# The last sort stage in two halves: the second half of the edges is finished between the one-hots of the first

## The chip, the cores and the metric

The kernel runs on one core of a Trainium2 chip. Its time is the device time of one execution in microseconds (us), as the median of several runs; a profile of one execution is read beside it. The engines are PE (matrix products), DVE (vector), ACT (activations, copies out of PSUM), POOL (here mostly issuing DMAs) and SP (issuing DMAs).

## What is computed

A graph layer without its nonlinearity: 4096 nodes of 256 features and 262,144 edges.

```python
self_out = nodes @ w_self
msg = nodes[edges_src] @ w_msg
agg = zeros(N, D); np.add.at(agg, edges_dst, msg)
return self_out + agg
```

As `nodes[src] @ w_msg` is row `src` of `Y = nodes @ w_msg`, the work is `A @ Y + nodes @ w_self`, where `A[dst, src]` counts the edges from `src` to `dst`. The kernel builds the counts `A` in tiles and multiplies them.

## The kernel before

**Load and key (L155 to L182).** The edges come in as 128 rows of 2048. DVE makes one f32 key of each edge: its destination segment (11 of them, 374 nodes each), its source block (32 blocks of 128 nodes), the destination in the segment and the source in the block. A pair of segment and block is called a run; there are 352.

**First sort (`SORT_A`, `_Sort.run`, tiles XA).** A network of compare-exchange passes along the rows. One pass is a `min` and a `max` on DVE (`_Sort.mm`, L634). Between groups of passes PE rotates columns across partitions (L777), and ACT copies the result back (L781). The last rotation of the list is applied by the transposes that follow.

**Last sort stage (`SORT_S`, tiles XS, L823 to L847).** PE transposes 28 blocks of 128 x 128, and ACT copies them to XS (L834), so that partition q holds columns 16q to 16q+15 of the sorted order, 2048 elements, with a halo of 768 of its neighbours' elements on either side. 16 passes then run along the partition, each narrower than the last, with no exchange between partitions. `_tail_plan` works out the ranges, and `waves` starts the first two passes on the part that has already come. Ahead of these passes PE and ACT are given the projection `Y` (L230), which runs beside them.

**Bases and places (L257 to L306).** For each of the 2048 columns of 128 sorted edges DVE finds the smallest key (`k16`, `gi`), and subtracts this base from the column's keys (`rel`). PE transposes `rel` (L280), and ACT turns it into 16-bit `vals`, one column of 128 edges per free index (L283). DVE works out from `gi` in which PSUM bank and at which offset each column's counts go (`poff`); 10 small steps. An ACT pass sums whatever falls outside the width W (L304).

**Main loop (L464 to L512).** It goes over the 2048 columns, and the order of the instructions on every engine is the order of the Python text (`manual_schedule`). For each block of columns (8, 8, 16, 32, 32, 32, then 64 each) DVE writes two one-hot tiles, `e_oh` (source in block, 128 wide) and `d_oh` (destination, W = 112 wide), with three buffers each (L333 to L352): one subtraction (L344) and then one comparison for every 16 values of the width (L349). For each column PE multiplies the two and adds the product at a run-time offset in a ring of six PSUM banks:

```python
count_mm(
    ring[:, bass.ds(off, W)], e[:, ci // 2, :, ci % 2], d[:, ci // 2, :, ci % 2], False
)
```

The keys are near enough to sorted that run r falls between two straight lines in the column number: `CLEAR` says at which column its bank is cleared (L384, it waits for the copy out of run r-6), and `EVAC` at which column ACT copies it to SBUF (L393). 46 columns later three products with `Y` add it to `out_ps` (L438 to L442). Where a count falls over the end of its segment, POOL adds the overhang to the next run by an accumulating DMA (`merge`, L411). After 32 runs a segment of the output is complete; ACT copies it to one of two `o_sb` buffers, and SP stores it in pieces, each of which waits for a later run's copy (L507).

**Check (L515 to L541).** The bases are written to DRAM and read back shifted by one (`kd`, `kn`, on SP), and DVE sees whether any column lies outside what the ring can hold. If one does, a general path is taken (`_any_edges`); on the data of this case it is not. These steps stand behind the manual order; they are placed where the scheduler puts them: in the program before, SP issues both DMAs ahead of all stores, and DVE runs the steps (L523 to L531) between the first blocks of one-hots.

Of the kernel before, what the change touches and what calls it, by code (L numbers as in the profile page):

```python
# [9 lines left out]
P = 128  # L10
# [12 lines left out]
W = 112  # L23
GAP = W - 8
NB = 32
JB = 16
NSEG = 11
# [36 lines left out]
    ('q', 2, [64, 91, 42, 124, 107, 2, 87, 24, 28, 87, 6, 7, 86, 49, 10, 1]),  # L64
# [12 lines left out]
def kernel(  # L77
# [17 lines left out]
    G16 = NCOL // P  # L95

# [14 lines left out]
    nc.gpsimd.iota(col_i[:], pattern=[[1, G16]], base=0, channel_multiplier=G16)  # L111
# [12 lines left out]
    TOT = NCOL + 2 * halo  # L124
# [22 lines left out]
    muladd(lom_c[:], lo_c[:], 683, 0)  # L147
    tss(out=lom_c[:], in_=lom_c[:], scalar=12, op=ALU.logical_shift_right)
    muladd(lom_c[:], lom_c[:], RING, -OFF)
    muladd(hi_c[:], hi_c[:], 1, -OFF)  # L150
# [90 lines left out]
    sort = _Sort(nc, tc, psum_sort, XA, XS, id2, zw)  # L241
    own = sort.run(plan, halo, project)

    def col16(name, dt):
# [9 lines left out]
    junk = meta.tile([P, NCOL], BF16, name="junk")  # L254
    bcol = meta.tile([P, 2], FP32, name="bcol")

    other = XS[0] if own is XS[1] else XS[1]  # L257
    own = own[:, halo:halo + NCOL]
    rel = other[:, 0:NCOL]
    assert SORT_S[-1] == (8, 1)  # L260
    low8 = own.rearrange("p (c i t b) -> p c i t b", i=8, t=2, b=8)
    sort.note(
        nc.vector.tensor_reduce(out=k16[:], in_=low8[:, :, :, 1, :], axis=AX.XY, op=ALU.min), NCOL // 2
    )
    sort.note(
        nc.vector.tensor_reduce(out=kmin[:], in_=low8[:, :, 0, 0, :], axis=AX.X, op=ALU.min), NCOL // 16
    )
    sort.note(tt(out=k16[:], in0=k16[:], in1=kmin[:], op=ALU.min), G16)
    sort.note(tss(out=gi[:], in_=k16[:], scalar=7, op=ALU.arith_shift_right), G16)
    sort.warm(len(sort.log), 2.4, 9)  # L270
    for t in range(G16 // 4):
        tp = psum_sort.tile([P, 512], FP32, name="tp_sw", tag="tp", bufs=4)
        s4 = slice(4 * t * P, 4 * (t + 1) * P)
        stt(
            out=_view3(rel[:, s4], P), in0=_view3(own[:, s4], P), scalar=1.0 / P,
            in1=gi[:, 4 * t:4 * t + 4].unsqueeze(2).to_broadcast([P, 4, P]),
            op0=ALU.mult, op1=ALU.subtract,
        )
        for k in range(4 * t, 4 * t + 4):
            nc.tensor.transpose(  # L280
                tp[:, (k % 4) * P:(k % 4 + 1) * P], rel[:, k * P:(k + 1) * P], ident[:]
            )
        nc.scalar.activation(  # L283
            out=vals[:].rearrange("p (q k) -> p q k", k=G16)[:, :, 4 * t:4 * t + 4],
            in_=tp[:].rearrange("p (k q) -> p q k", k=4),
            func=ACTF.Relu, scale=-float(P), bias=top[:],
        )
    muladd(rho[:], gi[:], 1.0 / SW, 0.5 / SW - 0.5)
    stt(out=dl[:], in0=rho[:], scalar=float(-SW), in1=gi[:], op0=ALU.mult, op1=ALU.add)
    tt(out=rhoc[:], in0=rho[:], in1=lo_c[:], op=ALU.max)  # L290
    tt(out=rhoc[:], in0=rhoc[:], in1=hi_c[:], op=ALU.min)
    tt(out=sl[:], in0=rhoc[:], in1=lom_c[:], op=ALU.subtract)
    nc.vector.tensor_scalar(
        out=wr[:], in0=sl[:], scalar1=float(RING), scalar2=float(-RING * BW),
        op0=ALU.is_ge, op1=ALU.mult,
    )
    stt(out=wr[:], in0=sl[:], scalar=float(BW), in1=wr[:], op0=ALU.mult, op1=ALU.add)
    tt(out=poff[:], in0=wr[:], in1=dl[:], op=ALU.add)
    nc.vector.tensor_scalar(
        out=poff[:], in0=poff[:], scalar1=2, scalar2=PSUM0,  # L300
        op0=ALU.logical_shift_left, op1=ALU.bitwise_or,
    )
    sort.keep_warm(10)
    nc.scalar.activation(  # L304
        out=junk[:], in_=vals[:], func=ACTF.Relu, scale=-1.0, bias=limit[:], accum_out=bcol[:, 1:2],
    )  # L306
# [16 lines left out]
    split_at = {0: 64, 64: 512, 512: 1280, 1280: NCOL}  # L323
# [4 lines left out]
    def onehots(c, n):  # L328
        res = []
        if c in split_at:  # L330
            split_vals(c, split_at[c])
        for nm, val, wid, row in (("e", slo_b, P, jrow), ("d", rel_b, W, drow)):
            o = ohp.tile([P, 32, wid, 2], BF16, name=nm + "_oh", tag=nm, bufs=3)  # L333
            v = val[:, c:c + n].rearrange("p (g i) -> p g i", i=2).unsqueeze(2)
            if n < 32:
                shp = [P, n // 2, wid, 2]
                tt(
                    out=o[:, 0:n // 2], in0=v.to_broadcast(shp),
                    in1=row[:].unsqueeze(1).to_broadcast(shp), op=ALU.is_equal,
                )  # L340
            else:
                u = ohp.tile([P, 32, JB, 2], I16, name=nm + "_off", tag="off", bufs=2)
                shp = [P, n // 2, JB, 2]
                tt(  # L344
                    out=u[:, 0:n // 2], in0=v.to_broadcast(shp),
                    in1=row[:, 0:JB, :].unsqueeze(1).to_broadcast(shp), op=ALU.subtract,
                )
                for j in range(0, wid, JB):
                    tss(  # L349
                        out=o[:, 0:n // 2, j:j + JB, :], in_=u[:, 0:n // 2], scalar=float(-j),  # L350
                        op=ALU.is_equal,
                    )  # L352
            res.append(o)
        return res
# [28 lines left out]

    def clear(r):  # L384
        b = (r % RING) * BW
        after = [evac_of[r - RING]] if r >= RING else []
        zone = bass.AP(
            tensor=ring.tensor, offset=ring[:, b:b + 1].offset,
            ap=[list(ring[:].ap[0]), [SW + W - GAP, 2], [1, GAP]],
        )  # L390
        count_mm(zone, zer[:, 0, :], zer[:, 1:3, 0:GAP], True, after)

    def evac(r):  # L393
        at = ats[r % NAT]
        b = (r % RING) * BW
        ins = nc.scalar.copy(out=at[:, 0:SW + W], in_=ring[:, b:b + SW + W]).ins  # L396
        tc.declare_no_dep(
            ins, group="count", keep=[last_mm[0]], reason="disjoint banks by static schedule"
        )
        tc.add_manual_dep(ins, last_mm[0].name, DEP, reason="run complete")  # L400
        tc.add_to_no_dep_group("evac", ins)
        evac_of[r] = ins
        at_of[r] = at
# [60 lines left out]
    if True:  # L464
# [3 lines left out]
        nev = 0  # L468
        starts = {}
# [4 lines left out]
        for c in range(NCOL):  # L474
            if c in starts:
                c0 = c
                e, d = onehots(c, starts[c])
            ci = c - c0
            while ncl < NRUN and clear_at(ncl) <= c:
                clear(ncl)  # L480
                ncl += 1
            if c % 8 == 0:
                regs = [nc.tensor.alloc_register(f"po{c}_{i}") for i in range(8)]
                nc.tensor.load(regs, poff[c // G16:c // G16 + 1, c % G16:c % G16 + 8])
# [33 lines left out]
    bsum = meta.tile([1, 2], FP32, name="bsum")  # L518
    btot = meta.tile([1, 1], FP32, name="btot")
    flag = meta.tile([1, 1], I32, name="flag")  # L520
    nc.sync.dma_start(kd[0, 0:NCOL].rearrange("(p g) -> p g", g=G16), k16[:])
    nc.sync.dma_start(kn[:], kd[0, 1:NCOL + 1].rearrange("(p g) -> p g", g=G16))
# [9 lines left out]
    nc.tensor.matmul(out=ring[0:1, 0:2], lhsT=onesc[:], rhs=bcol[:], start=True, stop=True)  # L532
    nc.vector.tensor_copy(out=bsum[:], in_=ring[0:1, 0:2])  # L533
    tt(out=btot[:], in0=bsum[:, 1:2], in1=bsum[:, 0:1], op=ALU.add)
    nc.vector.tensor_single_scalar(out=flag[:], in_=btot[:], scalar=0.0, op=ALU.is_gt)
    ohp.release()
    psum2.release()
# [62 lines left out]
def _tail_plan(passes):  # L600

    a, e = 0, 2048
# [10 lines left out]
    halo = -(-max(-a, e - 2048) // 128) * 128  # L613
# [8 lines left out]
class _Sort:  # L622
    def __init__(self, nc, tc, psum, XA, XS, id2, zw):
        self.nc, self.tc, self.psum = nc, tc, psum
        self.XA, self.XS, self.id2, self.zw = XA, XS, id2, zw
        self.log = []
        self.turn = 0

# [3 lines left out]
    def mm(self, out, in0, in1, op):  # L632
        self.note(
            self.nc.vector.tensor_tensor(out=out, in0=in0, in1=in1, op=op),  # L634
            out.ap[1][1] * out.ap[2][1],
        )
# [149 lines left out]
    def run(self, plan, halo, project):  # L786
# [36 lines left out]
        u, v = self.XS  # L823
        nk = (2048 + 2 * halo) // P
        for t in range(0, nk, 4):
            w = min(4, nk - t)
            tp = self.psum.tile([P, 512], FP32, name="tp_sw", tag="tp", bufs=4)
            for k in range(t, t + w):
                c = k - halo // P
                nc.tensor.transpose(  # L830
                    tp[:, (k - t) * P:(k - t + 1) * P],
                    x[:, FP + c:FP + c + 16 * (P - 1) + 1:16], self.turned(last[c // 2 % 8]),
                )
            nc.scalar.copy(out=u[:, t * P:(t + w) * P], in_=tp[:, 0:w * P])  # L834
        project()
        waves = []
        for end in (1024, 2048):
# [7 lines left out]
        return self.passes(  # L845
            u, v, [q[0:2] for q in plan], halo, [q[2:4] for q in plan], waves
        )[0]  # L847
# [30 lines left out]
```

## Time and profile before

| what | number |
|---|---|
| median of 5 runs | 484.07 us (483.16 to 486.45) |
| profiled execution | 487.51 us, of which the span of the profile is 485.7 |
| mean granted PE clock | 0.943 |
| first sort, DVE XA group (142 instructions) | 97.1 us busy |
| last sort stage, DVE XS group (40 instructions) | 131.7 to 178.3 us |
| first one-hot on DVE | 184.6 us |
| one-hot products on PE (2048) | 186.6 to 474.8 us |

In a group of the page, the columns are line, engine, operation, output and input with partitions x elements, count; then busy us and mean ns of one; then the idle time of the engine just before and what ended most of it. In a table of windows, each engine has its busy us and count, and behind them stand the granted PE clock (1.00 is full), the share of the DMA engines and GB/s. In a list of waits: who waited for whom, us in total, times, longest. In a timeline: start, length, engine, line, operation, count.

### The profile page before, as it was taken

The page shows a single profiled execution, that of the slowest core. Times are in us where ns is not written, and L with a number is a line of the kernel's source. Part 1 is how long each engine was busy: PE and PEld are TensorE (multiplying, and loading weights), DVE is VectorE, ACT ScalarE, POOL GpSimd, SP SyncE. Part 2 cuts the span into 40 slices and gives each one's busy share as a digit, 9 for nine tenths or more (in the row PEclk, how much of TensorE's full clock was granted, in tenths as well). Part 3 has the DMA queues.
Part 4 walks back from the last instruction along what each step waited for, and adds up shares of the span by engine and source line. Part 5 has one row for each costly group of instructions (what it writes and reads, how often), then busy time and mean ns, then how long its engine had stood idle before and what let it go on. Part 6 is the DMA issues. An engine that isn't in the chain of part 4 may idle for free.

```text
span 485.7 us, 10912 instructions
## 1 busy us (share of the span) xinstructions
PE 373.9 (77%) x4086; PEld 305.7 (63%) x4095; DVE 402.2 (83%) x834; ACT 239.2 (49%) x454; POOL 195.6 (40%) x190
## 2 busy tenths in 40 slices
PE   0009746989870039989999999989999999989994
PEld 0004231655440015779888989879898899988893
DVE  6999999899899999999988768787988688986400
ACT  3100010322271005567676767667676677767772
POOL 4200000000000000566766577666667675766760
PEclk9999786999996559999999999999999999999998
DMA  8894111111000000334544444453545454545351
GB/s 323 117 168 119 27 24 27 26 25 27 11 0 0 0 1 2 26 27 38 52 40 51 42 49 44 46 50 40 53 42 55 39 55 39 56 38 54 37 58 43
DMA packets 66016, 23.90 MB, mean 49 GB/s; under 512 B 51882, under 2 KB 64682, under 8 KB 65962
## 3 DMA queue, kind: packets, MB, share of 16 engines
q0 software_dynamic: 43872, 10.57, 26.4%
q1 hardware_dynamic: 21260, 10.42, 8.1%
q10 hardware_dynamic: 830, 2.20, 1.2%
q8 instruction: 33, 0.54, 0.5%
q14 instruction: 21, 0.17, 0.1%
HBM read 8.92 MB, written 6.30 MB: 31 GB/s over the span
## 4 chain that ended last, share of the span: by engine, by line
PE 48%; DVE 29%; issue 7%; POOL 6%; DMA 6%; ACT 2%; SPq 0%; POOLq 0%; DVEq 0%; ACTq 0%
PE ring L372 20%; PE out_ps L439 18%; DVE XA L634 14%; DVE XS L634 10%; POOL atr L416 6%; PE warm L671 6%; DMA atr<-atr 4%; PE tp_sw L777 2%; DMA d<-in_edges_dst_dram 2%; PE out_ps L434 1%; PE out_ps L428 1%; DVE e_oh L349 1%; DVE d_oh L349 1%; ACT atr L396 1%; ACT XA L781 1%
## 5 line engine op out<-in xcount | busy, mean ns | idle before, releaser
L416 POOL DMA_DIRECT2D atr<-atr x163 | 186.9, 1269 | 267.7 <-ACT atr L396 264.6
L396 ACT CAST atr<-ring 128x486 bf16<-128x486 f32 x352 | 192.9, 567 | 89.7 <-PE ring L372 68.7
L372 PE MATMUL ring<-d_oh,e_oh 128*128 128x112 bf16 x2048 | 193.2, 213 | 8.7 <-issue 4.6
L439 PE MATMUL out_ps<-Y,atr 128*128 128x256 bf16 x1056 | 170.0, 272 | 4.6 <-DMA atr<-atr 4.2
L372 PEld LDWEIGHTS <-e_oh 128*128 128x128 bf16 x2048 | 162.0, 97 | 15.6 <-issue 6.4
L349 DVE TENSOR_SCALAR e_oh<-e_off 128x1024 bf16<-128x1024 int16 (+1 forms) x264 | 98.7, 444 | 39.0 <-PE ring L372 38.1
L671 PE MATMUL warm<-zw 128*128 128x512 bf16 x169 | 56.7, 432 | 86.5 <-DVE XA L634 50.9
L634 DVE TENSOR_TENSOR XA<-XA 128x510 f32<-128x510 f32 (+35 forms) x142 | 97.1, 732 | 6.2 <-ACT XA L781 4.5
L439 PEld LDWEIGHTS <-atr 128*128 128x128 bf16 x1056 | 89.3, 97 | 13.4 <-DMA atr<-atr 5.5
L671 PEld LDWEIGHTS <-zw 128*128 128x128 bf16 x176 | 17.8, 104 | 121.5 <-issue 59.4
L372 PE MATMUL ring<-zer 128*128 128x208 bf16 x352 | 88.3, 251 | 0.1
L349 DVE TENSOR_SCALAR d_oh<-d_off 128x1024 bf16<-128x1024 int16 (+1 forms) x231 | 87.1, 446 | 1.1
L781 ACT COPY XA<-tp_sw 128x512 f32<-128x512 f32 x24 | 14.2, 592 | 93.3 <-PE tp_sw L777 92.6
L634 DVE TENSOR_TENSOR XS<-XS 128x512 f32<-128x512 f32 (+17 forms) x40 | 46.0, 1196 | 2.6 <-ACT XS L834 2.0
L372 PEld LDWEIGHTS <-zer 128*128 128x128 bf16 x352 | 34.0, 97 | 3.6 <-ACT atr L396 1.5
L777 PEld LDWEIGHTS tp_sw<-XA,id 128*128 128x128 f32 x192 | 22.5, 190 | 3.3 <-ACT XA L781 1.7
L777 PE MATMUL tp_sw<-XA,id 128*128 128x128 f32 x192 | 23.4, 276 | 1.2 <-DVE XA L634 1.2
L344 DVE TENSOR_TENSOR e_off<-slo_b,jrow 128x1024 int16<-128x1024 int16 (+1 forms) x33 | 21.5, 653 | 0.0
L344 DVE TENSOR_TENSOR d_off<-rel_b,drow 128x1024 int16<-128x1024 int16 (+1 forms) x33 | 21.5, 652 | 0.0
L533 DVE COPY bsum<-ring 1x2 f32<-1x2 f32 x1 | 0.1, 148 | 24.1 <-PE ring L532 24.1
L283 ACT ACTIVATE vals<-tp_sw,top 128x512 int16<-128x512 f32 x4 | 2.4, 688 | 34.5 <-PE tp_sw L280 34.5
L434 PE MATMUL out_ps<-Y,atr 128*128 128x256 bf16 x65 | 17.6, 271 | 0.0
(95 smaller groups left out, 141.7 us busy)
## 6 DMA issues: line engine op xcount, KB each, us to landing
atr<-atr POOLq DMA_DIRECT2D x123, 56.0 KB, 2.8
out_dram<-o_sb SPq DMA_DIRECT2D x110, 32.0 KB, 1.5
nodes_bf<-in_nodes_dram POOLq DMA_DIRECT2D x1, 2048.0 KB, 16.3
nodes_bf_dram<-nodes_bf SPq DMA_DIRECT2D x1, 2048.0 KB, 8.7
atr<-atr POOLq DMA_DIRECT2D x40, 28.0 KB, 2.8
s<-in_edges_src_dram ACTq DMA_DIRECT2D x2, 512.0 KB, 8.8
d<-in_edges_dst_dram SPq DMA_DIRECT2D x2, 512.0 KB, 6.2
XT<-nodes_bf_dram SPq DMA_TRANSPOSE x64, 2.4
```

Of the source, the lines that this page charges most:

```text
L344: tt(out=u[:, 0:n // 2], in0=v.to_broadcast(shp), in1=row[:, 0:JB, :].unsqueeze(1).to_broadcast(shp), op=ALU.subtract,)
L349: tss(out=o[:, 0:n // 2, j:j + JB, :], in_=u[:, 0:n // 2], scalar=float(-j), op=ALU.is_equal,)
L372: mm = nc.tensor.matmul(out=ap, lhsT=lhsT, rhs=rhs, start=start, stop=True, skip_group_check=True,).ins
L396: ins = nc.scalar.copy(out=at[:, 0:SW + W], in_=ring[:, b:b + SW + W]).ins
L416: nc.gpsimd.dma_start(out=atr[:, b:b + n, 0:W], in_=atr[:, a:a + n, SW:SW + W], accum_op=ALU.add)
L428: nc.tensor.matmul(out=out_ps[0:m, t, :], lhsT=XT[:, k, c0:c0 + m], rhs=wcat[:, k, :], start=(k == 0 and t % 2 == 0), stop=False, skip_gro ...
L434: nc.tensor.matmul(out=out_ps[:, 0, :], lhsT=spill[:, SW:SW + P], rhs=Y[:, b, :], start=False, stop=False, skip_group_check=True,)
L439: nc.tensor.matmul(out=out_ps[:, t, :], lhsT=at[:, t * P:(t + 1) * P], rhs=Y[:, b, :], start=False, stop=(b == NB - 1), skip_group_check=True,
L634: self.nc.vector.tensor_tensor(out=out, in0=in0, in1=in1, op=op),
L671: self.nc.tensor.matmul(out=w[:], lhsT=self.zw[:, 0:P], rhs=self.zw[:], start=True, stop=True).ins
L777: self.nc.tensor.matmul(out=tp[:, g * P:(g + 1) * P], lhsT=self.turned(rots[8 * h + 4 * t + g]), rhs=sel(x)[:, 4 * t + g], start=True, sto ...
L781: self.nc.scalar.copy(out=sel(y)[:, 4 * t:4 * t + 4], in_=tp[:].rearrange("p (g i b) -> p g i b", g=4, b=bb),)
```

## The change

The last sort stage is done in two halves of 1024 columns. Each half is transposed to its own pair of tiles with its own halos of 768 (20 blocks each: XS, and the new XL), so that partition q holds columns 8q to 8q+7 of the half. The passes of the first half stay where they were. Those of the second are kept as a list of 32 instructions, which are issued four at a time after the one-hots of each block from column 256 on. After the one-hots of block 768 the second half's bases and subtractions follow; its transposes go to one bank of the ring, which is lent out between runs 147 and 148, in the middle of the columns 857 and 872; the later runs all move on by one bank (`bank`, `bank_free`). The second half's places are worked out ahead of block 960, and its values are split at column 1024.

```diff
-W = 112
+W = 110
+HALF = 1024
+SHIFT = 148
+LATE_FROM = 256
+LATE_STEP = 4
+LATE_SUB = 768
+LATE_TURN = 872
+LATE_USE = 960
...
-    ('q', 2, [64, 91, 42, 124, 107, 2, 87, 24, 28, 87, 6, 7, 86, 49, 10, 1]),
+    ('q', 2, [103, 74, 61, 94] * 4),
...
-    TOT = NCOL + 2 * halo
+    TOT = HALF + 2 * halo
+    latep = tc.alloc_tile_pool(name="latep", bufs=1)
+    XL = [latep.tile([P, TOT], FP32, name=f"XL{i}") for i in range(2)]
...
+            if self.h == 0:
+                stt(
+                    out=sl[:, c], in0=rhoc[:, c], scalar=float(SHIFT - OFF), in1=sl[:, c],
+                    op0=ALU.is_ge, op1=ALU.add,
+                )
...
-    split_at = {0: 64, 64: 512, 512: 1280, 1280: NCOL}
+    split_at = {0: 64, 64: 512, 512: HALF, HALF: HALF + 256, HALF + 256: NCOL}
...
+    def bank(r):
+        return (r + (r >= SHIFT)) % RING * BW
+
+    def bank_free(slot):
+        old = slot - RING
+        if old == SHIFT:
+            return [late_read[-1]]
+        return [evac_of[old - (old > SHIFT)]] if old >= 0 else []
...
+    def turn_late(t):
+        b = bank(SHIFT - 1) // BW
+        b = (b + 1) % RING * BW
+        mms, act = late.turn(t, ring[:, b:b + BW])
+        for m in mms:
+            after = bank_free(SHIFT) if t == 0 else [late_read[-1]]
...
     def clear(r):
-        b = (r % RING) * BW
-        after = [evac_of[r - RING]] if r >= RING else []
+        b = bank(r)
+        after = bank_free(r + (r >= SHIFT))
...
+                if c == LATE_USE:
+                    late.places()
                 e, d = onehots(c, starts[c])
+                if c >= LATE_FROM:
+                    for _ in range(LATE_STEP):
+                        if rest:
+                            rest.pop(0)()
+                if c == LATE_SUB:
+                    assert not rest
+                    late.bases()
+                    for t in range(2):
+                        late.subtract(t)
+            if c == LATE_TURN:
+                turn_late(1)
+                late.total()
             ci = c - c0
             while ncl < NRUN and clear_at(ncl) <= c:
+                if ncl == SHIFT:
+                    turn_late(0)
                 clear(ncl)
...
-    nc.sync.dma_start(kd[0, 0:NCOL].rearrange("(p g) -> p g", g=G16), k16[:])
-    nc.sync.dma_start(kn[:], kd[0, 1:NCOL + 1].rearrange("(p g) -> p g", g=G16))
+    for h in range(2):
+        nc.sync.dma_start(
+            kd[0, h * HALF:(h + 1) * HALF].rearrange("(p g) -> p g", g=G8), k16[:, h * G8:(h + 1) * G8]
+        )
+    for h in range(2):
+        nc.sync.dma_start(
+            kn[:, h * G8:(h + 1) * G8],
+            kd[0, h * HALF + 1:(h + 1) * HALF + 1].rearrange("(p g) -> p g", g=G8),
+        )
...
+        own = self.passes(*self.XS[0], ps, halo, spans, waves)[0]
+        self.defer = []
+        self.passes(*self.XS[1], ps, halo, spans, [])
+        late, self.defer = self.defer, None
```

`late.turn(t, tp)` transposes four blocks of 128 x 128 f32 on PE into `tp` and lets ACT write `vals` from it, `late.bases` is the two reductions and two small steps of L262 to L269, `late.subtract(t)` is one instruction of L274, `late.places` the small steps of L288 to L302, and `late.total` the sum of L304 over one half. In the built program the second half's check steps (`gn` and `v`) stand on DVE within block 832, the others within the places at block 960; on SP, the first half's `kd` stands ahead of all stores, and the second half's `kd` and both `kn` after the third store of the third segment.

## The prediction

> **What bounds the kernel now.** I read the page first.
>
> ```profile
> PE 373.9 (77%) x4086; PEld 305.7 (63%) x4095; DVE 402.2 (83%) x834; ACT 239.2 (49%) x454; POOL 195.6 (40%) x190
> ...
> PE 48%; DVE 29%; issue 7%; POOL 6%; DMA 6%; ACT 2%; SPq 0%; POOLq 0%; DVEq 0%; ACTq 0%
> ...
> L349 DVE TENSOR_SCALAR e_oh<-e_off 128x1024 bf16<-128x1024 int16 (+1 forms) x264 | 98.7, 444 | 39.0 <-PE ring L372 38.1
> ...
> L634 DVE TENSOR_TENSOR XS<-XS 128x512 f32<-128x512 f32 (+17 forms) x40 | 46.0, 1196 | 2.6 <-ACT XS L834 2.0
> ```
>
> DVE is busiest, yet PE holds the chain. Two stages with different limits explain it. The table by windows:
>
> ```profile
> 150.00:160.00 10.00, 0.00 (x0) 0.00 (x0) 9.90 (x8) 0.00 (x0) 0.00 (x0) 0.52 0.00 0
> 160.00:170.00 10.00, 0.00 (x0) 0.00 (x0) 9.86 (x9) 0.00 (x0) 0.00 (x0) 0.50 0.00 0
> ...
> 220.00:260.00 40.00, 38.69 (x514) 35.88 (x511) 37.63 (x97) 28.92 (x54) 26.61 (x24) 1.00 0.45 44
> 260.00:300.00 40.00, 38.12 (x504) 34.92 (x503) 30.52 (x76) 27.59 (x52) 27.22 (x24) 1.00 0.48 48
> ```
>
> From 131.7 to 178.3 us the last sort stage runs on DVE with nothing beside it: every microsecond removed there is one of the span. From 186.6 to 474.8 PE is nearly full, and DVE is idle a quarter of the time only from about 260 us; before, it is full. The waits say the same: DVE waits for PE to free one-hot buffers, PE hardly waits for DVE.
>
> ```profile
> DVE e_oh L349 <- PE ring L372: 38.1, 23, 3.5
> ...
> PE ring L372 <- DVE d_oh L349: 2.8, 2, 2.0
> ```
>
> The sum hangs on how far DVE is ahead when the late sort begins. From the DVE timeline:
>
> ```profile
> 178.22 1.21 DVE L263 TENSOR_REDUCE k<-XS 128x16 int32<-128x1024 f32 x1
> ...
> 180.08 2.50 DVE L274 SCALAR_TENSOR_TENSOR XS<-XS,gi 128x512 f32<-128x512 f32 x4
> ...
> 189.35 0.17 DVE L523 TENSOR_SCALAR gn<-kn 128x16 int32<-128x16 int32 x1
> ...
> 216.77 0.68 DVE L344 TENSOR_TENSOR e_off<-slo_b,jrow 128x1024 int16<-128x1024 int16 x1
> ...
> 224.11 0.68 DVE L344 TENSOR_TENSOR e_off<-slo_b,jrow 128x1024 int16<-128x1024 int16 x1
> ```
>
> The line at 216.77 opens the one-hots of block 256 (columns 256 to 319); they end at 224.18. Counting the 2048 one-hot products on PE, column 256 starts at 227.32: a lead of 3.1 us. The leads at blocks 320, 384, 448, 512 and 832 are 4.6, 6.8, 9.7, 10.2 and 11.4 us. So the idle 38 us belong to a DVE that already has its three buffers full, which is later than where the late sort is put.
>
> **Ahead of the first one-hot.** The pass pairs fit n/0.96 ns plus 0.131 us (n = 1040: 1.160 and 1.269 us from start to start). Every one of the 16 passes loses 1024 elements (3584 to 2560 columns with halos) and the instructions stay 40: 16,384 x 1.0417 ns = 17.07 us. The reductions halve: 0.53 + 0.07. Two of four subtractions go: 1.25; the address steps stay ten on DVE (the added bank-shift step replaces one check that ran there), and two ACT turnings still end before them. Sum 18.9 us, all on the path. The 12 more transposes and 3 more ACT copies come ahead of the projection, which ended at 147.2; with 10 x 0.5 us of ACT instead of 7 it ends near 149, under a sort that now ends at 161. If that cover were gone they would cost 1.5 us.
>
> The first blocks are bound by DVE (leads 0.05 us at columns 64 and 128). Five small check steps (the line at 189.35 and four like it) leave this stretch: 0.8 us. d one-hots of 110 save 0.2. Block 256's one-hots therefore end at 224.18 - 19.9 = 204.3.
>
> **The late sort.** 23,408 elements x 1.0417 ns + 32 x 0.131 = 28.6 us, in eight portions of four instructions after the one-hots of blocks 256 to 704: 5.3, 4.7, 3.8, 3.4, 3.2, 3.0, 2.8, 2.7. A one-hot block takes DVE 6.96 us (mean distance of five starts from 202.89 to 237.69), 6.93 at the new width; PE takes 8.2 to 9.9. So DVE gains some 2 us a block on PE and the portions take more. The lead of 3.1 us is gone at block 320 (3.1 + 8.2 - 12.2 = -0.9). From there to block 832 DVE sets the time, with PE idle by about 0.9, 3.0, 2.3, 2.6, 1.7, 1.5, 1.2, 1.2 us a block.
>
> After block 768 come the late reductions and subtractions, 2.5 us, and then a new wait. gn (after block 832's e_off) needs kn, which needs kd's second half: in the trace kn's last packet landed 2.7 us after k was done; one more issue ahead of it (0.33) makes 3.1, of which 2.1 pass in DVE work. I take 1.0 us; bounds 0 and 2.5, if busy DMA doubles the landings. Behind it on DVE stand the one-hots of block 832, for which PE waits. On SP, the second kd and both kn stand ahead of nine stores of the third segment: these are held until k is done, some 120 columns, then go in a burst; their buffer is not needed before column 989, so 0, or up to 1 us if the burst delays merges.
>
> DVE from 204.3: nine blocks 62.4 + late sort 28.6 + splitting values 0.4 + 2.5 + wait 1.0 + gn, v 0.3 = 95.2, so block 832 is ready at 299.5. PE began it at 307.36 before. Of 19.9 us gained, 12.1 are given back: 7.8 stay.
>
> **Turning the late half.** Both turnings lie in block 832, now on PE's path: eight f32 transposes at 145 ns (16 took 2.32 in L280) are 1.16. ACT gets two activations of 0.6 and a sum over 1024 of about 1.0 (2.00 for 2048 at L304). The borrowed bank leaves five for the ring: five clears wait for the copy that was issued 8 columns earlier instead of 14. The one at column 881 waits for a copy that stands behind turning and sum on ACT: 2.7 us after the turn, where PE arrives after 1.0; 1.7, plus 0.3 for the others. No row shows this; bounds 1.2 (all ACT hidden) and 4.5 (the other four clears also 0.3 late and the copies bunched). I take 3.2, as this ACT copy row (0.56) and the columns give it.
>
> Width 110: in the trace products of 112 start 50 ns apart, 256-wide ones 108: 0.4 ns a column, 0.8 us per 1000 products. From column 832: 1216 x 0.8 ns = 1.0, and 203 clears narrower by four columns 0.35. The earlier part is bound by DVE, where it buys nothing. -1.35; bounds 0 and -2.
>
> **A rule against the change.** The Trainium skill, "TensorE: Matmul & The Clock Gate" (Why this matters for your kernels), allows no PE gaps over some 3 us between bursts, or the clock falls to half. My gap at block 384 is 3.0. The trace: PE's work ended at 146.85 and the clock fell at about 150.4 (0.52 in the first window above), after 3.5 us; the 2.03 us below left it at 1.00.
>
> ```profile
> 207.92 0.26 PE L372 MATMUL ring<-d_oh,e_oh 128*128 128x112 bf16 x2
> 210.21 0.26 PE L372 MATMUL ring<-d_oh,e_oh 128*128 128x112 bf16 x2 [2.03 <-DVE d_oh L349]
> ```
>
> By the row nothing is lost; by the rule one re-warming at half clock (its 3.4 us, so an estimate of 1.7 us), which fits in the 2 us PE is waiting anyway. I take 0.
>
> **Sum.** -7.8 + 3.2 - 1.35 = -5.95 us. The profiled execution took 487.51 (span 485.7 and 1.8 around it), 0.7% above the median 484.07; carried over unscaled: 478.1.
>
> **Rivals.**
> - Everything hides: DVE's 44 us idle between 220 and 460 exceed the 33 added, and nothing comes late. 484.07 - 19.9 + 3.2 - 2.2 (width over all products) = 465.2. The totals speak for it, the lead of 3.1 us against: 6%.
> - DVE is slower with the sort in between: if every block takes the 7.34 of block 256 rather than 6.93, nine blocks cost 3.7 more; with 4.5 for the turning, 483.1. The later blocks of the trace, their waits taken out, lie near 7.1. 17%.
> - Slower: the clock falls in the gaps of 2.3 to 3.0 us (blocks 384 to 512) and doesn't recover there. A block of 8.2 becomes 16.4 against 10.6 of DVE: three blocks x 5.8 = 17.4, 495.5. It decides where a gap comes to some 3.2 us. Against it: PE only 75% busy between 204 and 212 us at clock 1.00. 9%.
> - That the late half isn't taken off the path: the order of DVE instructions shows its passes only from block 256 on. Under 1%.
>
> **Numbers.** The main case holds 68%, 474.5 to 482: turning 1.2 to 4.5, wait 0 to 2.5, DVE block 6.7 to 7.1. A measurement of this kernel tells about 0.5% from no change (481.7 to 486.5). Faster: main case and first rival, 0.74; same 0.17; slower 0.09. The range 474.5 to 484 takes in the second rival and leaves out the first and third.
>
> **What would show it.** First one-hot near 165.7 us; the XS group near 29 us and an XL group of 32 near 29; PE waiting for DVE one-hots 10 to 15 us in all, none after block 832, and DVE almost without idle up to there; a DVE wait of about 1 us before gn; ring clears waiting for ACT near column 881; the clock at 1.00. It is wrong if leads stay positive through block 320 (then nearer 465), or if the clock falls, or if the first one-hot isn't 19 us earlier.

## The result and the profile after

The changed kernel takes 483.13 us (median of 42 runs) against 484.08 (79 runs): ratio 0.998, 95% interval 0.9966 to 0.9994. Timed twice more, on two chips, it gave 0.9984 (0.9962 to 1.0005) and 0.9983 (0.9958 to 1.0007). The gain is near 1 us, where 6 were forecast. Single executions of either kernel scatter by about 1.7 us (standard deviation; one of the 42 took 589 us, at a granted clock of 0.67, and is left out of this and of the ratio). That matters below: the profile of the changed kernel happens to be of an execution of 481.69, 1.4 below its median, and that of before was 3.4 above its own.

The page after, for the lines that were shown of before:

```profile
PE 379.0 (79%) x4098; PEld 310.3 (65%) x4107; DVE 416.1 (87%) x884; ACT 240.5 (50%) x459; POOL 196.0 (41%) x190
...
PE 46%; DVE 45%; DMA 4%; issue 2%; ACT 2%; SPq 0%; DVEq 0%; ACTq 0%
...
L402 DVE TENSOR_SCALAR e_oh<-e_off 128x1024 bf16<-128x1024 int16 (+1 forms) x264 | 99.8, 448 | 17.7 <-PE ring L425 15.5
...
L749 DVE TENSOR_TENSOR XS<-XS 128x512 f32<-128x512 f32 (+17 forms) x40 | 28.9, 770 | 2.6 <-ACT XS L950 2.0
L746 DVE TENSOR_TENSOR XL<-XL 128x1196 f32<-128x1196 f32 (+15 forms) x32 | 28.1, 919 | 0.3
```

DVE's share of the chain went from 29% to 45%: 17 us left the XS group, and 28 came back as XL, with DVE's wait for PE more than halved (38.1 to 15.5). The table by windows:

```profile
150.00:160.00 10.00, 0.26 (x1) 0.28 (x3) 9.76 (x15) 0.00 (x0) 0.00 (x0) 0.52 0.00 0
160.00:170.00 10.00, 9.09 (x50) 4.82 (x50) 9.32 (x26) 3.13 (x6) 0.00 (x0) 0.79 0.01 2
220.00:260.00 40.00, 33.01 (x414) 30.21 (x412) 39.33 (x80) 23.45 (x44) 23.91 (x22) 0.96 0.38 38
260.00:300.00 40.00, 35.37 (x445) 32.50 (x445) 37.57 (x87) 24.08 (x46) 21.99 (x19) 0.96 0.38 35
```

The sort alone with DVE is shorter, and between 220 and 300 us PE and DVE have changed roles: PE is busy 68 us of 80 instead of 77, DVE 77 instead of 68, and the clock is no longer at 1.00. The waits name who is late:

```profile
PE ring L425 <- DVE d_oh L402: 16.2, 10, 3.2
...
DVE e_oh L402 <- PE ring L425: 15.5, 11, 3.5
...
DVE gn L633 <- DMA kn<-kd: 1.7, 1, 1.7
...
PE ring L425 <- ACT atr L481: 1.3, 1, 1.3
```

PE waited 2.8 us for `d_oh` before and waits 16.2 now. The ten waits come about one to a block. On DVE's timeline the first of them is seen coming: four instructions of the late sort (two passes), 5.2 us, lie between the one-hots of block 256 and those of block 320.

```profile
205.21 5.22 DVE L746 TENSOR_TENSOR XL<-XL 128x1196 f32<-128x1196 f32 x4
210.35 0.68 DVE L396 TENSOR_TENSOR e_off<-slo_b,jrow 128x1024 int16<-128x1024 int16 x1
```

The stages of several profiles, counted from the products on PE and the one-hot blocks on DVE (us from the start of the span):

| profile | first one-hot | block 256 ready | column 832 on PE | last product | from 832 to the end of products |
|---|---|---|---|---|---|
| before | 184.6 | 224.2 | 307.4 | 474.8 | 167.5 |
| before, 2nd | 184.6 | 224.3 | 306.5 | 473.4 | 166.9 |
| before, 3rd | 183.4 | 222.9 | 303.3 | 469.3 | 166.1 |
| after | 166.1 | 205.3 | 302.3 | 469.0 | 166.7 |
| after, 2nd | 165.2 | 204.2 | 302.3 | 471.6 | 169.3 |
| after, 3rd | 164.6 | 203.9 | 300.8 | 467.4 | 166.7 |
| after, 4th | 166.1 | 205.4 | 303.9 | 472.0 | 168.1 |

### The profile page after: what moved, and what is told of

It is laid out like the page before. It is cut to its first block, busy times and chain, and to the rows that moved or that the text cites. A ratio compares the mean times of both kernels' runs of the same rounds, so it can differ in the third digit from the quotient of the medians.

```text
span 479.9 us, 10985 instructions
## 1 busy us (share of the span) xinstructions
PE 379.0 (79%) x4098; PEld 310.3 (65%) x4107; DVE 416.1 (87%) x884; ACT 240.5 (50%) x459; POOL 196.0 (41%) x190
## 4 chain that ended last, share of the span: by engine, by line
PE 46%; DVE 45%; DMA 4%; issue 2%; ACT 2%; SPq 0%; DVEq 0%; ACTq 0%
PE ring L425 18%; PE out_ps L524 15%; DVE XA L749 15%; DVE e_oh L402 9%; DVE d_oh L402 8%; PE warm L786 6%; DVE XS L749 6%; DVE XL L746 4%; PE tp_sw L892 2%; DMA d<-in_edges_dst_dram 2%; DVE d_off L396 2%; DVE e_off L396 1%; PE out_ps L519 1%; DMA atr<-atr 1%; PE out_ps L599 1%
## 5 line engine op out<-in xcount | busy, mean ns | idle before, releaser
L481 ACT CAST atr<-ring 128x484 bf16<-128x484 f32 x352 | 192.3, 565 | 101.4 <-PE ring L425 82.2
L425 PE MATMUL ring<-d_oh,e_oh 128*128 128x110 bf16 x2048 | 195.9, 215 | 19.0 <-DVE d_oh L402 16.2
L425 PEld LDWEIGHTS <-e_oh 128*128 128x128 bf16 x2048 | 163.7, 98 | 24.4 <-issue 14.6
L402 DVE TENSOR_SCALAR e_oh<-e_off 128x1024 bf16<-128x1024 int16 (+1 forms) x264 | 99.8, 448 | 17.7 <-PE ring L425 15.5
L524 PEld LDWEIGHTS <-atr 128*128 128x128 bf16 x1056 | 90.5, 97 | 8.0 <-DMA atr<-atr 1.6
L425 PE MATMUL ring<-zer 128*128 128x204 bf16 x352 | 88.3, 251 | 1.4 <-ACT atr L481 1.3
L402 DVE TENSOR_SCALAR d_oh<-d_off 128x1024 bf16<-128x1024 int16 (+3 forms) x231 | 86.4, 444 | 1.1
L749 DVE TENSOR_TENSOR XS<-XS 128x512 f32<-128x512 f32 (+17 forms) x40 | 28.9, 770 | 2.6 <-ACT XS L950 2.0
L746 DVE TENSOR_TENSOR XL<-XL 128x1196 f32<-128x1196 f32 (+15 forms) x32 | 28.1, 919 | 0.3
## 6 DMA issues: line engine op xcount, KB each, us to landing
nodes_bf<-in_nodes_dram POOLq DMA_DIRECT2D x1, 2048.0 KB, 16.2
```

Source lines behind the costliest of these rows:

```text
L402: tss(out=o[:, 0:n // 2, j:j + w, :], in_=u[:, 0:n // 2, 0:w, :], scalar=float(-j), op=ALU.is_equal,)
L425: mm = nc.tensor.matmul(out=ap, lhsT=lhsT, rhs=rhs, start=start, stop=True, skip_group_check=True,).ins
L524: nc.tensor.matmul(out=out_ps[:, t, :], lhsT=at[:, t * P:(t + 1) * P], rhs=Y[:, b, :], start=False, stop=(b == NB - 1), skip_group_check=True,
L746: self.defer.append(lambda: self.nc.vector.tensor_tensor(out=out, in0=in0, in1=in1, op=op))
```

## The experiments

My theory after the result (A): the steps hold, but before was measured in an execution whose products ran slowly, so the late sort seemed to have more room than it has. The rival (B): the changed kernel's other executions are worse than its profiled one, through falls of the clock. Further ones came with the runs.

**Both kernels again.** No edit.

> The kernel before, unchanged, for a second profile. Theory A (the forecast's steps hold, but the profiled execution of before that they were made against was a slow one: its product stream on PE ran slower than usual, so that in a usual execution the late sort has less slack to hide in): first one-hot again at 184.6 us, but PE reaches column 832 about 2 us earlier than the 307.4 of the first profile and ends near 471 to 473; span about 482. Theory B (before was as usual, and the executions of the changed kernel are mostly worse than its profiled one): span near 485 with the same stage table as the first profile.

> The kernel before, for a third profile, beside its own timed runs. Theory A: an execution near the median of its chip reaches column 832 near 305 and ends its products within 287 us of the first (288.2 and 286.8 in the two slow profiles).

> The changed kernel, unchanged, for a second profile. Theory A: the same stage table as its first profile up to column 832, where DVE sets the time (within 1 us of 302.3), and a span of 480 to 482. Theory B: two to four more clock falls in the gaps from block 384 on, column 832 later than 304 us, span 483 or more.

Before took 486.06 and 482.0 us: the second profile reached column 832 at 306.5, where I expected some 305.4, the third (303.3) went beyond my expectation. The three executions lie within 1.4 us of each other up to block 256; from column 256 to column 832 PE then needs 80.0, 79.9 and 77.5 us. The changed kernel's second (484.27) reached 832 at 302.3 as the first had, and lost its 2.6 us behind it, 1.7 of them in block 832, where the clock fell at 303.4. So both theories are right in part.

**The width.**

```diff
-W = 110
+W = 112
```

> The changed kernel with the width back at 112. By the forecast's step the narrower width is worth 1.35 us past column 832 and nothing ahead of it, where DVE sets the time, but for 33 ns of DVE a block: 1.4 to 2 us slower than the changed kernel, ratio to before 1.001 to 1.002. If the narrow tiles themselves hurt (rows of 440 bytes in place of 448 for DVE's writes and PE's reads), it is faster than the changed kernel by 1 us or more.

483.46 us, ratio 0.9935 (0.9913 to 0.9958), on a chip where before took 486.47 and a single execution of the changed kernel 484.27: not slower, as I had expected it to be. The median distance from one one-hot product to the next is 51 ns at both widths, and that of a clear to the next product went from 88 to 87. The 0.4 ns a column that I had taken between widths of 112 and 256 isn't there between 110 and 112. The mean even goes the other way: from column 832 on, over the distances of 44 to 58 ns, it is 51.7 ns in each of the four profiles at 110 and 51.2 in the four at 112 (the three of before and this one), some 0.6 us over 1216 products. Set against before, this run is 2 us faster than the changed kernel (0.9935 against 0.998), but the two were timed on different chips, and their profiles take 301.3 and 301.0 us for the products. Whether the narrow tiles cost more than the 0.6 us stays open.

**The late passes, none and half.** Both leave the second half of the edges unsorted, and the fallback is off (`scalar=1e30` in the last comparison).

```diff
-        rest = sort.late
+        rest = []
```

> The changed kernel without the 32 late sort passes (the second half stays unsorted, and the fallback is switched off); everything else stays, the late reductions, the turning and the check steps too. Theory A and B alike by the forecast: DVE keeps its lead, PE reaches column 832 some 12 us earlier than with the passes (about 290), and the time is 470 to 472, ratio 0.972 to 0.976. Rival (the give-back lies elsewhere, in the turning or in the bank that is lent out): 480 or more.

467.16 us, ratio 0.9617 (0.9582 to 0.9651), column 832 at 286.3, 4 us earlier than expected. 27.7 us of DVE work cost 16 us of time. With 16 of the 32 instructions, two a block (`rest = sort.late[8:24]`, `LATE_STEP = 2`):

> The changed kernel with 16 of the 32 late sort instructions (passes 5 to 12 of 16, 13.0 us of DVE of 27.7), two a block; the second half stays unsorted and the fallback is switched off. Without any of them the time was 467.2 and column 832 came at 286.3, with all of them some 483 and 302. If DVE has room for a fixed amount and only what is beyond it is paid (204.5 + 9 x 7.1 + 4.8 + 13.0 = 286.2 against PE's own 286.3), half of the passes cost nearly nothing: column 832 at 286 to 288, 467 to 469. If the passes cost PE in proportion (by ports or memory beside its products), 475.

467.26 us, ratio 0.968 (0.9636 to 0.9724), column 832 at 286.1. The two ratios, on different chips, leave 0 to 3 us for the half; the column says 0. In proportion it would have been 7. The window from block 256 to column 832 of this second kernel shows how close both engines are to full at once:

```profile
205.00:286.00 81.00, 78.42 (x1028) 72.09 (x1026) 77.67 (x180) 57.31 (x110) 54.03 (x48) 1.00 0.47 46
```

DVE has room for some 12 us up to there: the 16 instructions took 12.3 us, counted as the 27.7 are, and leave DVE no lead at column 832. What is beyond is paid in full: all 32 took 15.4 us more, and PE reached column 832 15.2 us later after block 256 (97.0 against 81.8, first profile of the changed kernel). Ports or memory beside PE's products play no part that can be seen.

**The check steps.** Their DMAs are put at column 960 and their DVE steps at 1536, by hand:

```diff
                 if c == LATE_USE:
                     late.places()
+                    check_load()
                 e, d = onehots(c, starts[c])
+                if c == 1536:
+                    check_steps()
```

> The changed kernel with its check steps written into the order by hand: both kd and both kn on SP at column 960, the DVE steps at column 1536 where DVE is ahead. It takes the wait for kn and the two steps behind it out of block 832, 1.7 + 0.3 us in the profile. If DVE sets the time up to block 832, column 832 comes 2.0 us earlier and the time falls by 1.5 to 2.5 us against the changed kernel. If PE or its clock sets it there, nothing.

> The changed kernel, unchanged, timed beside the kernels below on one chip, and a third profile. From the profiles so far (column 832 at 302.3 in three of three, against 306.5 and 307.4 before; the rest of the stream equally long) 3 to 5 us faster than before, ratio 0.990 to 0.994. If the first timing (0.998) is the truth for every chip: 0.996 to 1.0.

> The changed kernel unchanged, timed beside its edit with later check steps on one chip, for their difference: ratio to before 0.996 to 0.999 as in its two timings.

> The edit with later check steps again, beside the changed kernel on one chip. If its gain of 2.7 us (7 runs) was not chance of these few runs: 2 us faster than the changed kernel, as the 2.0 us that the DVE timeline of block 832 loses say; ratio 0.992 to 0.995.

The two pairs, each on one chip: 483.09 (22 runs) and 480.36 (7), 483.74 (22) and 480.31 (15). The edit gains 2.7 and 3.4 us, more than the 2.0 of the timeline; ratio to before 0.9918 (0.9886 to 0.995) and 0.9916 (0.9892 to 0.9939). The changed kernel itself missed the 0.990 to 0.994 that I expected of after_timed. Its fourth profile (484.67 us, near the median) shows why the edit is worth more. DVE:

```profile
293.78 0.68 DVE L396 TENSOR_TENSOR e_off<-slo_b,jrow 128x1024 int16<-128x1024 int16 x1
297.51 0.17 DVE L633 TENSOR_SCALAR gn<-kn 128x16 int32<-128x16 int32 x1 [3.05 <-DMA kn<-kd]
```

PE at the same place:

```profile
300.27 0.49 PE L524 MATMUL out_ps<-Y,atr 128*128 128x256 bf16 x3
303.86 0.26 PE L425 MATMUL ring<-d_oh,e_oh 128*128 128x110 bf16 x2 [3.10 <-DVE d_oh L402]
```

And the windows on both sides of column 832 (the last three numbers are clock, DMA share and GB/s):

```profile
300.00:304.00 4.00, 0.90 (x14) 0.70 (x12) 3.96 (x11) 1.03 (x2) 3.29 (x3) 1.00 0.54 67
304.00:307.60 3.60, 3.60 (x30) 3.01 (x29) 3.49 (x10) 1.12 (x2) 0.00 (x0) 0.53 0.16 22
```

The wait for kn took 3.0 us here (1.7, 2.6 and 1.7 in the other three): kd's write took 2.8 us from issue to release kn's, where it took 1.4 in the first profile. It makes PE's gap ahead of column 832 3.1 us long, and 0.2 us later the clock falls to half for 3.4 us. This is in the block in which PE, not DVE, sets the time: it took 12.35 us against 10.4 in the first profile. The second profile, with 2.6 us of waiting, shows the same fall. A longer wait is paid twice: once as such, and once by the fall, some 2 us in two of four profiles. That and the 2.0 of the timeline make about 3.

**PE kept busy.** 6 to 14 products of zeros (256 wide) after the last column of the blocks 256 to 768:

```diff
+            for _ in range(IDLE.get(c + 1, 0)):
+                nc.tensor.matmul(
+                    out=out_ps[:, 3, :], lhsT=zw[:, 0:P], rhs=zw[:, 0:D], start=False, stop=True,
+                    skip_group_check=True,
+                )
```

> The changed kernel with 6 to 14 idle products of zeros (256 wide, added to an unused quarter of out_ps) after the last column of each block from 256 to 768, where PE waits for DVE anyway. The granted clock stays at 1.00 from 164 us to the end (in the profiles it fell once or twice, to half for 3.4 us). Theory B (clock falls are what the other executions lose by): 1 to 3 us faster than the changed kernel. Theory A: the falls are mostly hidden by DVE, 0 to 1.2 us faster.

481.76 us (22 runs) beside 483.09: 1.3 us faster, ratio 0.9952 (0.9934 to 0.9969), and no fall of the clock. So the falls cost the changed kernel some 1.3 us, roughly, as the two intervals still touch (the other is 0.9962 to 1.0005). It fits a fall of some 2 us in every second execution. Both edits at once:

> The changed kernel with both edits at once: check steps at columns 960 and 1536, and idle products where PE waits for DVE. If their gains lie on one chain and add (2.7 and 1.3 us against the changed kernel at 483.1), 479 and ratio 0.989 to 0.991; if the clock falls only where the kn wait makes a gap, no better than the check steps alone (480.4, 0.992).

482.01 us, 0.9951 (0.9931 to 0.9971): a miss. The gains don't add; once the wait for kn is gone, the fillers give nothing. The profile reaches column 832 at 299.9, as with the check steps alone (299.9 and 300.1), and loses its time behind column 896, where no filler stands: 158.9 us to the last product against 156.2 and 155.5. Why stays open (another chip, too).

**An uneven split.** 1536 and 512 columns: less is taken off the path, but the late half has 15,216 elements, two instructions a block, and is used at column 1536. The core of the edit:

```diff
-HALF = 1024
+HALF = 1536
+REST = 512
...
-LATE_STEP = 4
-LATE_SUB = 768
+LATE_STEP = 2
+LATE_SUB = 1280
...
-LATE_USE = 960
+LATE_USE = 1472
```

> The same idea with 1536 and 512 columns in place of 1024 and 1024: the late sort has 15,216 elements (20 us), issued two instructions a block over 16 blocks from column 256, used at column 1536, turned in one step near column 1313. The early sort saves only 8192 elements (8.5 us) and 0.9 in reductions and subtractions. If what failed is that the late work comes faster than DVE gains on PE, this hides it all: 1.3 us a block against 2; no wait of PE for DVE after block 256, and 484 - 9.4 - 0.8 (checks) - 2 (width) + 1.3 (turning) = 473, ratio 0.976 to 0.982. If DVE work between the one-hots costs PE time in itself (through ports, or DVE's rate), it stays near 0.995.

486.95 us, ratio 1.0066 (1.0043 to 1.0089): a miss, though DVE's lead never fell below 3 us after block 256. The stream of products was 297.3 us long. I had cut PE's loads of the offsets into pieces of 8 and 4 columns, as a partition now holds 12 or 4: 384 loads instead of 256. To see whether these do it, 12 and 4 at once:

> The uneven split again, with PE's offsets loaded into 12 registers at once for the first 1536 columns and 4 for the rest: 256 loads as in the changed kernel, where the uneven kernel had 384. If its long product stream (297.3 us against 287 to 288 before, with PE never waiting for DVE) came from the 128 more loads, the stream comes back to 288 to 290 and the time is 475 to 479. If it came from DVE's sort passes beside PE, or from 1536 columns of DVE lead lost, it stays at 487.

483.93 us, 1.0001 (0.9977 to 1.0024), stream 294.5: mostly a miss. The changed kernel with four columns a load:

> The changed kernel with its offsets loaded four columns at a time, 512 loads in place of 256, and nothing else. If a load costs PE 0.08 us (10 us over the uneven kernel's 128), up to 20 us slower, the more past column 832, where PE sets the time: some 14 us, 497. If loads are free behind PE's queue, 483.

496.07 us, 1.0255 (1.0206 to 1.0303): 12 to 13 us for 256 more loads. From column 832 on the products took 181.6 us instead of 167 to 169. Its waits, "issue" being time without a wait that the profile shows:

```profile
PEld L425 <- issue: 22.3, 39, 2.3
...
PE ring L425 <- issue: 12.2, 18, 1.5
```

The changed kernel has 20.9 and 1.3 us in these rows. What counts seems to be the number of loads near each other: with 12 and 4 at once the last 512 columns, 16 loads a block, took 75.4 us, where the changed kernel took 69.5 to 70.6. So the uneven split got its offsets through DRAM in one row, eight to a load:

```diff
+            nc.sync.dma_start(pd[self.h][0, :].rearrange("(p g) -> p g", g=self.g), poff[:, c])
+            nc.sync.dma_start(prow[self.h][:], pd[self.h][:])
...
+                nc.tensor.load(regs, prow[h][0:1, k:k + 8])
```

> The uneven split (1536 and 512 columns), with the offsets brought by DMA over DRAM into one row, so that PE loads eight at a time as in the changed kernel, 256 loads. If the loads of 4 and 12 are what lengthened the stream of both uneven kernels, it comes back from 294.5 and 297.3 to 286 to 288 us, and with a first product at 177 to 178 the time is 475 to 478, ratio 0.98 to 0.987. If the late passes or the turning lengthen it, 482 or more.

477.07 us (6 runs), ratio 0.9844 (0.9808 to 0.9881), the stream 287.8 us, the last 512 columns 70.8. It beats both kernels (the changed one took 483.74 on the same chip). Its waits show the same kinds as before:

```profile
DVE gn L642 <- DMA kn<-kd: 3.3, 1, 3.3
...
PE ring L436 <- DVE e_oh L400: 2.6, 1, 2.6
...
PE ring L436 <- DVE d_oh L413: 1.0, 1, 1.0
```

kn is waited for as long as ever, but DVE is still 10 us ahead after it, and PE doesn't notice.

## Why the prediction was wrong

The direction was right, and so was the mechanism: DVE's lead is used up, and most of what was gained ahead of the loop is given back. As a forecast of the time it was wrong by 5 us, by two steps: the base that the sum was taken from, and the length of the late stretch. That the sum agrees with the two profiled executions (-5.95 forecast, -5.8 us between their spans) is luck: column 832 came 5.1 us earlier in place of 7.8, and the stretch behind it took 0.8 us less in place of 1.85 more.

- **Ahead of the first one-hot: right.** 165.7 forecast, 164.6 to 166.1 measured. Block 256 ready: 204.3 against 203.9 to 205.4. The 12 more transposes and the projection stayed under the sort.
- **The base: the step that failed first.** "Carried over unscaled" set -5.95 against the median, though the profiled execution was 3.4 us above it. That is no neutral choice when one side is set by DVE and the other by PE. PE's column 832 of before enters the gain directly; DVE's of after doesn't depend on PE. Over three profiles before reaches 832 at 305.7, not 307.4: 1.7 us less to gain.
- **The late stretch, 95.2 us: too short.** 97.0, 98.0, 96.8 and 98.4 in the four profiles, so +2.4. In it, sort passes 27.7 us (28.6 forecast), one-hot blocks 7.13 (6.93) or +1.8, and the wait for kn 1.7 to 3.0 (1.0; my upper bound was 2.5) or +1.3. The gaps ahead of blocks 320 to 768 (0.8 to 1.1, 3.2, 0.5 to 2.8, ...) came where they were expected. (PE's blocks of before take 8.0 to 9.9 us, not 8.2 to 9.9, which changes little.)
- **The clock, taken at 0: wrong, about 1 us.** The row of 3.5 us against the Trainium skill's rule ("TensorE: Matmul & The Clock Gate", Why this matters for your kernels: no gaps over some 3 us between bursts): the rule came nearer, though seven falls here came at gaps of 2.2 to 2.8 us, under it. The row, of a gap of 31 us, could only say that 3.5 us is enough. In the first after profile, ahead of block 384:

```profile
225.58 0.25 PE L425 MATMUL ring<-zer 128*128 128x204 bf16 x1
228.98 0.43 PE L425 MATMUL ring<-d_oh,e_oh 128*128 128x110 bf16 x3 [3.15 <-DVE d_oh L402]
```

  A gap of 3.15 us, and the clock fell at 228.97. As forecast, that fall is hidden by DVE (block 384 took 10.65 us, DVE needed 11.1 for the next). So is the one in block 576: PE comes 1.1 us late to column 640, but column 704 stands 76.2 to 76.4 us behind block 256 in the three profiles with it and 76.5 in the one without. The one in block 832, which comes with a long wait for kn in two of the four profiles, has no cover and costs 1.7 and 1.9 us. I had looked for cover at one gap only.
- **The turning, 3.2: too long, but inside its bounds.** With eight transposes and one wait of PE for ACT (1.3 us, 1.7 forecast) PE takes 10.6 us from column 832 to column 896, where before took 8.1 to 8.2: 2.4 us. With the fall of the clock it is 12.2 and 12.5.
- **The width, -1.35: wrong, 0 or slightly the other way.** Products of before stand 51 ns apart in the median, not 50.
- **Behind column 896: a gain that was not forecast.** The four profiles take 156.2 us from there to the last product on average, before 158.7. All of these 2.5 us are shorter pauses of PE, 3.2 us in place of 5.7. Two kinds hold it: pauses without a wait that the profile shows, and waits for the DMAs that add the overhangs (atr). In the first profile of before and of after, over the whole span:

```profile
PE ring L372 <- issue: 4.6, 10, 1.1
...
PE out_ps L439 <- DMA atr<-atr: 4.2, 7, 1.1
```

```profile
PE ring L425 <- issue: 1.3, 5, 0.4
PE out_ps L524 <- DMA atr<-atr: 1.3, 2, 1.1
```

  Why PE pauses less, no run here shows. It is hardly the width: in the profile at 112 the pauses behind column 896 are 3.7 us.
- **Together.** Past column 832 the four profiles took 167.7 us on average, before 166.8: +0.9 instead of +1.85, as the turning and the fall in block 832 cost 3.3 and PE's shorter pauses gave 2.5 back. So the profiles' means give -3.4 + 0.9 = -2.5 us, and the timed runs -1.0. The rest, 1.5, is once more which executions were profiled: the three of before average 485.2 us, 1.1 above the median, and the four of after 482.7, 0.4 below theirs.

Of the rivals, "everything hides" fell by 16 us for the passes, and holds for half of them. "DVE is slower" was half right: 7.13 us a block, between 6.93 and 7.34. The clock fell, but came back after 3.4 us each time, so its rival didn't happen.

## What to carry to other kernels

Room on an engine is what it has before the deadline of the moved work: the lead at the place of insertion, and what it gains per step from there on. Count that, not the idle time of the whole stage; here it was some 12 us of 44, and work beyond it was paid in full. A gain of one per cent can't be read against one profile: take several of the kernel before, above all when the change makes another engine set the time. A round trip by DMA on an engine that sets the time belongs where that engine is ahead.

## What the runs showed of the hardware that was not expected

- Products of 110 and of 112 columns follow each other at the same median of 51 ns, with a weight load for each, while 256-wide ones take 108 to 109. The mean is 51.7 ns at 110 and 51.2 at 112.
- The falls of the clock in the one-hot loop keep to a beat, and each lasted one: within a profile its changes lie whole multiples of 3.41 us apart (228.97 and 263.10 in the first after profile are ten). Laid over PE's busy time in all 18 profiles, the beat tells which gaps matter: the clock fell after each of the 15 stretches of 3.41 us in which PE was busy for 1.40 us or less, and after none in which it was busy for 1.55 us or more. (PE's ends are modelled, so the line is rough; ahead of the loop one fall came at 1.60.) So the length of a gap alone doesn't decide, but how it lies on the beat: in the loop the clock fell at 8 of 8 gaps of 3.1 to 3.2 us, at 4 of 6 of 2.8, at 3 of 8 of 2.2 to 2.4, and at none of the three of 2.0 in the profiles of before.
- Loads of registers by PE are not free: 512 of four values instead of 256 of eight cost 12 to 13 us, some 0.05 us each, and near 0.09 where PE sets the time.
- A small write to DRAM in the full main loop took 1.4 to 2.8 us to release the read behind it.
